# A two-layer diffusion step on one core: weight loads and modulation loads in buffers of their own, and where the dot products stand

## The chip, the core and the metric

The kernel runs on one core of one Trainium2 chip. Five engines matter here: TensorE (PE in the rows; PEld is its weight load), VectorE (DVE), ScalarE (ACT), GpSimd (POOL) and SyncE (SP), whose only work is to issue loads. Each engine takes its instructions in program order and waits on semaphores. The metric is the device time of one execution, in microseconds (us), the median of several runs. GB in rates are 10^9 bytes; a MiB is 1,048,576 bytes.

## The reference

One step of a backbone with two layers, on 128 context tokens and 128 latent tokens, all in float32. D_MODEL is 2048 and D_FF 5632. What each layer computes:

```
m = silu(cond) @ w_mod_l + b_mod_l          # shift1, scale1, gate1, shift2, scale2, gate2
h = rms_norm(x) * (1 + scale1) + shift1
q_r, k_r, v_r, g_r, q_a, k_a, v_a = split(h @ w_in_l)     # 8 retention heads, 8 attention heads on 2 key heads
y = concat(retention_output(...), attention(...))
x = x + gate1 * (y @ w_out_l)
h = rms_norm(x) * (1 + scale2) + shift2
x = x + gate2 * ((silu(gate) * val) @ w_down_l)           # gate, val: depthwise conv of h @ w_up_l
```

The modulation m has six vectors of 2048 for each layer and token kind, so w_mod is 2 x 2048 x 12288 numbers: it is read once, for two columns of cond. After both layers there is one more norm with a gain. Outputs are the tokens and the new key, value and state caches.

## The kernel before

**Pieces.** All 256 tokens stay on chip, transposed. `build_work` (L47) cuts the four weight matrices of each layer into 128x128 tiles and lists them in the order of use, in 768 pieces of eight tiles (`PIECE`). For a piece, `split_upto` (L461) makes hi (ACT, L469) and lo (DVE, L470) from the raw float32 tiles, and `triple` (L635) multiplies each tile three times (L637 to L639), so a piece is 24 matmuls of 256 columns. Splits run `LOOK` = 3 pieces ahead of PE, in four hi and four lo buffers.

**Stages.** In layer 0, pieces 0 to 47 form the wide start (eight head groups by quarters of the contraction), 48 to 87 finish the heads, 88 to 119 are the output projection, 120 to 383 the feed-forward block in thirds (up, down, three times). Layer 1 follows from 384, its output projection is 472 to 503. Beside the heads, attention and retention run as side tasks, a step after each piece (`kv_task`, `q_task`, `ret_task`), with small matmuls into tiles named aux.

**Modulation** is computed in two ways. On PE: `emit_mod` (L394) and `emit_modq` (L377) multiply cond with one unit of w_mod of 1 MiB into a tile md; units come in pairs. `QSTART` are the 32 units at the start, `PESEQ` 32 units in layer 0, `QMID` 16 units, and `QNORM` four units at each of three norms, between the parts of the norm. On DVE: `emit_dot` (L407) multiplies a 1 MiB unit with cond and sums along the row, once for each token kind (k = 0 and 1), so a unit has two dots; it writes its product to the tile hua, by which the rows name it. `DVESEQ` lists the 100 units that go this way.

**What sets the order.** `body` first writes a list of events: each piece, and after it the modulation units that `quota` (L168, from the table `knots`) grants, and the dots that `plan` grants. `plan` spreads the dots evenly up to their due piece over the pieces whose `room` is not zero: all from piece 48 on (`ahead`), without those around a norm. Then the list is emitted in that order on all engines.

**Loads.** `need` (L257) lists all loads, weights and modulation, in the order of first use, and `pump` (L315) issues them on SP in that order, into five buffers (`RAWB`) of 1 MiB: a weight unit is sixteen tiles (`UNIT`), that is two pieces. A buffer comes free in `done` (L339), when its last reader has been emitted, and the load that takes it waits on SP for that reader; loads behind it on SP wait too.

Of the kernel before, what the change touches and what calls it, by code (L numbers as in the profile page):

```python
# [8 lines left out]
F32 = mybir.dt.float32  # L9
# [6 lines left out]
P = 128  # L16
D = 2048
KC = D // P
# [7 lines left out]
UNIT = 16  # L26
LOOK = 3
RAWB = 5
THIRDS = ((0, 16), (16, 16), (32, 12))
# [88 lines left out]

MU = KC * KC // UNIT

# [13 lines left out]
def body(ctx: ExitStack, tc: tile.TileContext, io):  # L134
    nc = tc.nc
# [119 lines left out]
    loads, where = [], {}  # L255

    def need(key):  # L257
        if key not in where:
            where[key] = len(loads)
            loads.append(key)  # L260

    sp = 0
    for ev, arg in events:
        if ev in ("mod", "modq"):
            need((ev, arg))
        elif ev == "dot":
            need(("dot", arg[:3]))
        elif ev in ("presplit", "piece"):
            upto = min(arg[0] + LOOK + 1 if ev == "piece" else arg, len(pieces))
            while sp < upto:  # L270
                need(("main", pieces[sp]["u"]))
                sp += 1
# [3 lines left out]
    wp = ctx.enter_context(tc.tile_pool(name="wp", bufs=RAWB))  # L276
    sp_ = ctx.enter_context(tc.tile_pool(name="split", bufs=LOOK + 1))
# [35 lines left out]
    raw, consumed, nload = {}, [0] * len(loads), [0]  # L313

    def pump():  # L315
        while nload[0] < len(loads):
            i = nload[0]
            if len(raw) >= RAWB:
                return
            key = loads[i]  # L320
            t = wp.tile([P, UNIT * P], F32, tag="raw", name="raw")
            if key[0] == "main":
                u = units[key[1]]
                n = u["n"] * P
                src = io[u["key"]][u["off"] * P * P:(u["off"] + u["n"]) * P * P]
                nc.sync.dma_start(t[:, :n], src.rearrange("(p f) -> p f", p=P))
            else:
                src = io["w_" + key[0]]
                if key[0] == "dot":
                    at = (DVESEQ.index(key[1]),)  # L330
                else:
                    at = ((PESEQ if key[0] == "mod" else QSEQ).index(key[1][:-1]), key[1][-1])
                for i in at:
                    src = src[i]
                nc.sync.dma_start(t, src)
            raw[key] = t
            nload[0] += 1

    def done(key):  # L339
        consumed[where[key]] = 1  # L340
        del raw[key]
        pump()
# [134 lines left out]
    def square(kc):  # L477

        x = xT[:, kc, :]
        if kc == 0:  # L480
            nc.scalar.activation(ssq, x, AF.Square)
        else:
            t = tp.tile([P, 256], F32, tag="t1", name="sq", bufs=4)
# [19 lines left out]
    def norm1():  # L503
        ps = aux()
        for s in range(2):
            for t in (ssq, diag[0]):
                nc.tensor.matmul(ps[:, s:s + 1], t[:, P * s:P * s + P], mean, start=t is ssq, stop=t is not ssq)
        ms = tp.tile([P, 2], F32, tag="ms", name="ms")
        nc.vector.tensor_scalar_add(ms, ps[:, 0:2], EPS)
        rs = tp.tile([P, 2], F32, tag="rs", name="rs")  # L510
        nc.gpsimd.tensor_tensor(rs, ms, mhalf, op=ALU.pow)
        dg = tp.tile([P, 256], F32, tag="t1", name="dg", bufs=4)
# [12 lines left out]
    def emit_hu(l, w, kcs, ahead=True):  # L525

        m = modT[l]
        for kc in kcs:
            if ahead:
                u = hua[:, kc % 4, :]  # L530
            else:
                u = tp.tile([P, 256], F32, tag="t1", name="hu", bufs=4)
# [228 lines left out]
    def layer_tables(l):  # L761
# [7 lines left out]
        for h in range(NH):  # L769
            t = tp.tile([P, 256], F32, tag="t1", name="dtmp", bufs=4)[:, 0:P]  # L770
# [121 lines left out]
    def ret_task(l, h, r):  # L892
# [53 lines left out]
        yf = tp.tile([P, 256], F32, tag="t1", name="ry", bufs=4)  # L946
# [65 lines left out]
def layout(inputs):  # L1012
# [18 lines left out]
    arrays["w_modq"] = np.stack([wm[l, :, :, :, v, b].transpose(0, 2, 1, 3).reshape(MU // 4, P, UNIT * P) for l, v, b in QSEQ])  # L1031
    wm = a["w_mod"].reshape(DEPTH, MU, KC // MU, P, 6, D)
    arrays["w_mod"] = np.stack([wm[l, :, :, :, v].transpose(0, 2, 1, 3).reshape(MU, P, UNIT * P) for l, v in PESEQ])
# [75 lines left out]
```

## Time and profile before

| | |
|---|---|
| median of 3 runs | 2460.34 us (2458.66 to 2462.38) |
| the profiled execution | 2464.25 us, of which its span 2462.4 us |
| PE busy | 2389.6 us (97%), 19730 instructions |
| DVE busy | 1842.0 us (75%) |
| ACT busy | 1201.9 us (49%) |
| moved by DMA | 619.38 MB, mean 252 GB/s |
| mean granted PE clock | 0.99 |
| DMA in the 40 slices, GB/s, first nine | 394 333 314 235 272 261 341 372 292 |

Half of the loads are weights (384 of 1 MiB), a quarter is modulation (192 of 1 MiB). Each slice is 61.6 us. A busy share is a mean over stages with different limits, so the stages are read one by one below. Pieces are counted by the matmuls of one line, eight to a piece.

### The profile page before, as it was taken

Reading aid. Unit: us, or ns where it says so; the run is one execution under the profiler, and the core shown is the slowest. Engines: PE = TensorE matmul, PEld = TensorE weight load, DVE = VectorE, ACT = ScalarE, POOL = GpSimd, SP = SyncE. Lnnn points to the kernel's source line nnn. Section 1 sums busy time; section 2 is a strip of 40 time slices with the busy share of each in tenths; the row PEclk is TensorE's granted clock in tenths of the full one; section 3 lists DMA queues with packets and bytes.
Section 4 is the critical chain, followed back from the end, with each engine's and each line's share of the span. In section 5 each row is a group of like instructions: output and inputs, shape, how many; then the busy total and the mean of one; then the engine's idle time right before and its main releaser. Section 6 shows DMA issues by size and latency. Waiting matters only on the chain.

```text
span 2462.4 us, 46787 instructions
## 1 busy us (share of the span) xinstructions
PE 2389.6 (97%) x19730; PEld 2289.1 (93%) x19730; DVE 1842.0 (75%) x2484; ACT 1201.9 (49%) x1896; POOL 24.7 (1%) x29
## 2 busy tenths in 40 slices
PE   6999989999999999999999999999999999999998
PEld 4888778789999999999989899998999999999997
DVE  4567777669998999889996878796997456655665
ACT  4534433355544555445556544456554454544554
POOL 0000000000000000000000000000000000000000
PEclk9999999999999999999999999999999999999999
DMA  9886778976777777777775687876676555555552
GB/s 394 333 314 235 272 261 341 372 292 239 258 272 261 266 260 258 272 262 264 262 270 208 217 296 289 297 272 227 226 286 217 185 185 187 189 182 187 185 183 86
DMA packets 91266, 619.38 MB, mean 252 GB/s; under 512 B 10160, under 2 KB 16304, under 8 KB 16944
## 3 DMA queue, kind: packets, MB, share of 16 engines
q1 hardware_dynamic: 83520, 605.21, 67.6%
q10 hardware_dynamic: 7536, 11.19, 1.2%
q8 instruction: 154, 2.52, 0.4%
q14 instruction: 56, 0.46, 0.0%
HBM read 611.64 MB, written 4.72 MB: 250 GB/s over the span
## 4 chain that ended last, share of the span: by engine, by line
PE 86%; DVE 6%; DMA 5%; ACT 2%; issue 1%; SPq 0%; POOL 0%; ACTq 0%; DVEq 0%; POOLq 0%
PE acc L637 27%; PE acc L639 27%; PE acc L638 27%; DMA raw<-in_w_modq 2%; DVE lo L470 2%; PE md L387 2%; DMA raw<-in_w_mod 2%; DVE hua L410 2%; ACT hi L469 1%; PE md L401 1%; ACT pr L833 1%; DMA raw<-in_w_in 0%; PE aux L861 0%; DVE st L825 0%; PE aux L442 0%
## 5 line engine op out<-in xcount | busy, mean ns | idle before, releaser
L470 DVE TENSOR_TENSOR lo<-raw,hi 128x1024 fp32r<-128x1024 f32 x768 | 934.6, 1222 | 373.2 <-ACT hi L469 370.3
L637 PE MATMUL acc<-hT,hi 128*128 128x256 f32 x4224 | 1203.0, 285 | 6.5 <-ACT hT L564 6.5
L638 PE MATMUL acc<-hT,hi 128*128 128x256 f32 x4224 | 1183.3, 280 | 0.8 <-DVE hT L569 0.8
L639 PE MATMUL acc<-hT,lo 128*128 128x256 f32 x4224 | 1182.7, 280 | 0.0
L469 ACT CAST hi<-raw 128x1024 fp32r<-128x1024 f32 x768 | 806.0, 1051 | 698.7 <-PE acc L638 585.8
L637 PEld LDWEIGHTS acc<-hT,hi 128*128 128x128 f32 x4224 | 797.8, 189 | 33.8 <-issue 18.3
L638 PEld LDWEIGHTS acc<-hT,hi 128*128 128x128 f32 x4224 | 795.5, 188 | 3.2 <-DVE hT L569 1.2
L639 PEld LDWEIGHTS acc<-hT,lo 128*128 128x128 f32 x4224 | 798.3, 189 | 0.0
L639 PE MATMUL acc<-ypair,lo 128*128 128x256 f32 x1920 | 543.7, 283 | 2.7 <-DVE lo L470 2.7
L637 PE MATMUL acc<-ypair,hi 128*128 128x256 f32 x1920 | 545.8, 284 | 0.0
L638 PE MATMUL acc<-ypair,hi 128*128 128x256 f32 x1920 | 543.3, 283 | 0.1
L410 DVE SCALAR_TENSOR_TENSOR hua<-raw,cbc 128x2048 bf16<-128x2048 f32 x200 | 456.7, 2284 | 6.6 <-DMA raw<-in_w_dot 6.6
L637 PEld LDWEIGHTS acc<-ypair,hi 128*128 128x128 f32 x1920 | 368.4, 192 | 8.6 <-issue 6.7
L639 PEld LDWEIGHTS acc<-ypair,lo 128*128 128x128 f32 x1920 | 368.3, 192 | 3.4 <-DVE lo L470 3.3
L638 PEld LDWEIGHTS acc<-ypair,hi 128*128 128x128 f32 x1920 | 368.4, 192 | 0.4 <-DVE ypair L758 0.3
L717 ACT ACTIVATE gx<-acc,modT 128x128 f32<-128x128 f32 x240 | 68.6, 369 | 94.8 <-PE acc L639 94.8
L719 DVE TENSOR_TENSOR xT<-gx,xT 128x512 f32<-128x512 f32 x60 | 41.4, 691 | 72.4 <-ACT gx L717 72.4
L387 PE MATMUL md<-raw,sc 128*32 128x512 f32 x480 | 65.8, 654 | 24.5 <-DMA raw<-in_w_modq 14.5
L746 DVE SCALAR_TENSOR_TENSOR cv<-acc,cst,cv 128x254 f32<-128x254 f32 x176 | 84.8, 482 | 6.2
L737 ACT ACTIVATE cv<-acc,cst 128x256 f32<-128x256 f32 x176 | 89.4, 558 | 0.0
L744 DVE SCALAR_TENSOR_TENSOR cv<-acc,cst,cv 128x254 f32<-128x254 f32 x176 | 83.4, 474 | 0.0
L387 PEld LDWEIGHTS md<-raw,sc 128*32 128x32 f32 x480 | 11.9, 113 | 53.1 <-DMA raw<-in_w_modq 28.4
(130 smaller groups left out, 922.7 us busy)
## 6 DMA issues: line engine op xcount, KB each, us to landing
raw<-in_w_up SPq DMA_DIRECT2D x176, 1024.0 KB, 4.9
raw<-in_w_dot SPq DMA_DIRECT2D x100, 1024.0 KB, 6.3
raw<-in_w_in SPq DMA_DIRECT2D x88, 1024.0 KB, 6.8
raw<-in_w_down SPq DMA_DIRECT2D x88, 1024.0 KB, 4.9
raw<-in_w_modq SPq DMA_DIRECT2D x60, 1024.0 KB, 7.0
raw<-in_w_mod SPq DMA_DIRECT2D x32, 1024.0 KB, 8.7
raw<-in_w_out SPq DMA_DIRECT2D x32, 1024.0 KB, 5.8
xT<-in_xT ACTq DMA_DIRECT2D x2, 1024.0 KB, 10.2
```

The lines of the kernel that those rows point to most:

```text
L387: nc.tensor.matmul(md[0][32 * j:32 * j + 32, :], sc[:, 2 * kc:2 * kc + 32], t[:, 512 * i:512 * i + 512], start=kc < 4, stop=kc >= 12)
L410: nc.vector.scalar_tensor_tensor(hua.rearrange("p c t -> p (c t)").bitcast(BF16), raw[key], 1.0, acc[:, k, :], op0=ALU.mult, op1=ALU.mult, ...
L469: nc.scalar.copy(hi, r)
L470: nc.vector.tensor_tensor(lo, r, hi.bitcast(F32), op=ALU.subtract)
L637: nc.tensor.matmul(out, hi, src[:, 0:256], start=first, stop=False, skip_group_check=True)
L638: nc.tensor.matmul(out, hi, src[:, 256:512], start=False, stop=False, skip_group_check=True)
L639: nc.tensor.matmul(out, lo, src[:, 0:256], start=False, stop=last, skip_group_check=True)
L717: nc.scalar.activation(tv[:, i, P * s:P * s + P], pv[:, i, P * s:P * s + P], AF.Copy, scale=modT[l][:, v, nt + i, s:s + 1])
L719: nc.vector.tensor_tensor(xT[:, nt:nt + 2, :], tv, xT[:, nt:nt + 2, :], op=ALU.add)
L737: nc.scalar.activation(t, src, AF.Identity, bias=C("convb", l * 2 * FC + f, 1), scale=w)
L744: nc.vector.scalar_tensor_tensor(t[:, :, 1:P], src[:, :, 0:P - 1], w[0], t[:, :, 1:P], op0=ALU.mult, op1=ALU.add)
L746: nc.vector.scalar_tensor_tensor(t[:, :, 0:P - 1], src[:, :, 1:P], w[2], t[:, :, 0:P - 1], op0=ALU.mult, op1=ALU.add)
```

## The change

Weight units shrink from sixteen tiles to eight (0.5 MiB, one piece) and keep their five buffers in the pool `wp`. Modulation units keep 1 MiB and get a pool of their own, `vp`, with three buffers (`MODB`), in tiles named vec. `pump` keeps two lists and fills the modulation buffers first; no weights are loaded before eight modulation units have been issued. To make room, the small temporaries of tag t1 go from four buffers to three (seven places, not shown again below). Dots start only at the output projection of layer 0 (`gstart["out", 0]`, piece 88). Four of their units (quarter 1 of layer 0's scale2, eight dots) go to PE: one more entry of `QMID`, four units, and the table `knots` grants them.

```diff
-UNIT = 16
+UNIT = 8
+MUNIT = 16
 LOOK = 3
 RAWB = 5
+MODB = 3
...
-QMID = [(0, 4, 0), (1, 2, 1), (1, 2, 2), (1, 2, 3)]
+QMID = [(0, 4, 0), (0, 4, 1), (1, 2, 1), (1, 2, 2), (1, 2, 3)]
...
-DVESEQ = [(l, v, u) for l, v, n in ((0, 4, 4), (0, 5, 4), (1, 1, 0), (1, 0, 0), (1, 4, 0), (1, 3, 0), (1, 5, 4))
+DVESEQ = [(l, v, u) for l, v, n in ((0, 4, 8), (0, 5, 4), (1, 1, 0), (1, 0, 0), (1, 4, 0), (1, 3, 0), (1, 5, 4))
...
-    knots = [(ahead, 0), (gstart["out", 0] - 2, MU), (gstart["up", 0] - 4, 9 * MU // 4), (gstart["kv", 1] + 16, 9 * MU // 4),
-             (gstart["out", 1] - 2, 3 * MU)]
+    knots = [(ahead, 0), (gstart["out", 0] - 2, MU), (gstart["up", 0] - 4, 5 * MU // 2), (gstart["kv", 1] + 16, 5 * MU // 2),
+             (gstart["out", 1] - 2, 13 * MU // 4)]
...
-        if j >= ahead and not ends:
+        if j >= gstart["out", 0] and not ends:
             room[j] = DSHARE[g["kind"]]
...
-    loads, where = [], {}
+    loads = {"main": [("main", i) for i in range(len(units))], "mod": []}
...
+    vp = ctx.enter_context(tc.tile_pool(name="vp", bufs=MODB))
...
-    raw, consumed, nload = {}, [0] * len(loads), [0]
+    raw, nload, held = {}, {"main": 0, "mod": 0}, {"main": 0, "mod": 0}
 
     def pump():
-        while nload[0] < len(loads):
-            i = nload[0]
-            if len(raw) >= RAWB:
-                return
...
+        while nload["mod"] < len(loads["mod"]) and held["mod"] < MODB:
+            key = loads["mod"][nload["mod"]]
+            t = vp.tile([P, MUNIT * P], F32, tag="vec", name="vec")
...
+        while nload["main"] < len(units) and held["main"] < RAWB and nload["mod"] >= MU // 2:
+            i = nload["main"]
+            u = units[i]
+            n = u["n"] * P
             t = wp.tile([P, UNIT * P], F32, tag="raw", name="raw")
...
     def done(key):
-        consumed[where[key]] = 1
+        held["main" if key[0] == "main" else "mod"] -= 1
         del raw[key]
         pump()
```

How loads stand on SP in the middle of layer 0's output projection, before (in_w_mod and in_w_modq are units for PE, in_w_dot units for DVE, in_w_out weights):

```order
L335 DMA raw<-in_w_mod 128x2048 x2
L326 DMA raw<-in_w_out 128x2048
L335 DMA raw<-in_w_dot 128x2048
L326 DMA raw<-in_w_out 128x2048
L335 DMA raw<-in_w_mod 128x2048 x2
L326 DMA raw<-in_w_out 128x2048
L335 DMA raw<-in_w_mod 128x2048 x2
```

The same place now:

```order
L323 DMA vec<-in_w_dot 128x2048
L323 DMA vec<-in_w_mod 128x2048 x2
L333 DMA raw<-in_w_out 128x1024 x3
L323 DMA vec<-in_w_mod 128x2048 x2
L323 DMA vec<-in_w_dot 128x2048
L333 DMA raw<-in_w_out 128x1024 x2
L323 DMA vec<-in_w_mod 128x2048 x2
```

Between two pairs for PE there stood one or two MiB of weights and at times a dot unit; now there stand two or three pieces of half a MiB, and a dot unit more often.

SP at the end of layer 1's output projection, where the norm takes four units (in_w_modq x4), before:

```order
L326 DMA raw<-in_w_out 128x2048 x3
L335 DMA raw<-in_w_dot 128x2048
L326 DMA raw<-in_w_up 128x2048 x2
L335 DMA raw<-in_w_modq 128x2048 x4
L326 DMA raw<-in_w_up 128x2048 x8
```

and now:

```order
L323 DMA vec<-in_w_modq 128x2048
L333 DMA raw<-in_w_out 128x1024 x3
L333 DMA raw<-in_w_up 128x1024 x2
L323 DMA vec<-in_w_modq 128x2048
L333 DMA raw<-in_w_up 128x1024 x6
L323 DMA vec<-in_w_modq 128x2048 x2
L323 DMA vec<-in_w_dot 128x2048 x2
```

The first two of the four units now stand ahead of weights of the next stage, the last two behind eight pieces of them.

DVE in a retention head of layer 0 (L936 sends a variance to POOL, L940 uses what comes back), before:

```order
L923 SCALAR_TENSOR_TENSOR ro<-aux,dec,ro 128x128 x2
L933 BN_STATS bs<-ro 128x6 x2
L935 BN_AGGR ag<-bs 128x2 x2
L936 TENSOR_SCALAR grs<-ag 128x2
L410 SCALAR_TENSOR_TENSOR hua,modT<-raw,cbc 128x2048
L470 TENSOR_TENSOR lo<-raw,hi 128x1024
L940 TENSOR_SCALAR ro<-ro,ag,grs 128x128 x2
```

and now:

```order
L922 SCALAR_TENSOR_TENSOR ro<-aux,dec,ro 128x128 x2
L932 BN_STATS bs<-ro 128x6 x2
L934 BN_AGGR ag<-bs 128x2 x2
L935 TENSOR_SCALAR grs<-ag 128x2
L469 TENSOR_TENSOR lo<-raw,hi 128x1024
L939 TENSOR_SCALAR ro<-ro,ag,grs 128x128 x2
```

The dot between the two is gone, and with it all 17 dots of pieces 48 to 87. After pieces 88 to 115 there are now 17 dots where there were 13, and 22 units for PE where there were 18; in the first up stage (pieces 136 to 183) there are 23 dots where there were 20. All later stages keep their numbers within one.

## Rows read from the trace of the kernel before

**Rows 1.** Stages: start:end, length; busy PE, PEld, DVE, ACT, POOL; clock, DMA share, GB/s.

```profile
33.20:204.20 171.00, 168.00 (x1368) 147.16 (x1369) 106.21 (x183) 78.97 (x110) 0.00 (x0) 0.97 0.88 334
204.20:386.90 182.70, 167.70 (x1298) 146.62 (x1296) 136.65 (x242) 74.03 (x144) 6.75 (x7) 0.98 0.68 251
386.90:497.70 110.80, 103.51 (x843) 87.37 (x840) 73.32 (x90) 41.24 (x72) 0.69 (x1) 1.00 0.96 374
571.70:707.40 135.70, 135.70 (x1155) 135.70 (x1154) 131.96 (x175) 71.22 (x101) 0.00 (x0) 1.00 0.74 264
```

**Rows 2.** The same view for line L639 alone: eight matmuls are one piece.

```profile
386.90:497.70 110.80, 63.14 (x224) 42.86 (x224) 1.00 0.96 374
799.50:980.50 181.00, 142.94 (x513) 96.25 (x512) 1.00 0.72 261
```

**Rows 3.** DVE in the dots (L410) alone, by stage; each dot has two records.

```profile
204.20:386.90 182.70, 36.66 (x32) 0.98 0.68 251
```

**Rows 4.** Timeline of the start: start, length, engine, line, operation, [idle before <- releaser].

```profile
29.08 1.07 PE L387 MATMUL md<-raw,sc 128*32 128x512 f32 x8 [1.42 <-DMA raw<-in_w_modq]
31.55 1.04 ACT L469 CAST hi<-raw 128x1024 fp32r<-128x1024 f32 x1 [0.75 <-DMA raw<-in_w_in]
31.77 0.17 DVE L371 TENSOR_TENSOR modT<-modT,cst 128x8 f32<-128x8 f32 x1
33.24 0.38 PE L637 MATMUL acc<-hT,hi 128*128 128x256 f32 x1 [1.73 <-ACT hT L564]
```

**Rows 5.** Timeline of the wide start around 65 us: loads issued, and PE's units.

```profile
54.92 0.80 SPq L335 DMA_DIRECT2D raw<-in_w_modq  x2
55.73 0.35 ACTq L425 DMA_DIRECT2D cbc<-in_cb  x1
64.89 1.06 PE L387 MATMUL md<-raw,sc 128*32 128x512 f32 x8
67.83 1.94 PE L387 MATMUL md<-raw,sc 128*32 128x512 f32 x8 [1.88 <-DMA raw<-in_w_modq]
```

**Rows 6.** Waits of PE in 204.2 to 386.9: who waited for whom, sum, times, longest.

```profile
PE aux L945 <- DVE ro L940: 5.8, 5, 2.2
PE aux L861 <- ACT pt L850: 2.7, 3, 1.8
PE aux L848 <- DVE pr L841: 2.6, 1, 2.6
```

**Rows 7.** Timeline of one retention head in that stretch.

```profile
336.30 2.28 DVE L410 SCALAR_TENSOR_TENSOR hua<-raw,cbc 128x2048 bf16<-128x2048 f32 x1
339.65 0.60 DVE L940 TENSOR_SCALAR ro<-ro,ag,grs 128x128 f32<-128x128 f32 x2
340.13 0.49 PE L945 MATMUL aux<-cst,ro 128*128 128x128 f32 x2 [2.15 <-DVE ro L940]
340.55 3.35 PE L401 MATMUL md<-raw,sc 128*32 128x512 f32 x16
```

**Rows 8.** Layer 0's output projection: PE's wait; bytes moved in 386.9 to 497.7.

```profile
PE md L401 <- DMA raw<-in_w_mod: 7.0, 6, 1.6
DMA packets 6114, 41.47 MB, mean 374 GB/s; under 512 B 684, under 2 KB 1113, under 8 KB 1113
```

**Rows 9.** Busy time by stage, 5 to 50 us, when loads queue without a gap.

```profile
5.00:50.00 45.00, 30.21 (x190) 17.23 (x191) 21.64 (x59) 19.52 (x40) 0.69 (x1) 0.92 1.01 421
```

**Rows 10.** Chain of waits: a load issued with nothing queued ahead, issue to landing.

```profile
1280.92 4.82 DMA raw<-in_w_modq
```

**Rows 11.** Timeline of the norms before layer 1 and before its feed-forward block.

```profile
1281.13 1.92 PE L387 MATMUL md<-raw,sc 128*32 128x512 f32 x16
1285.79 1.06 PE L387 MATMUL md<-raw,sc 128*32 128x512 f32 x8 [0.29 <-DMA raw<-in_w_modq]
1684.00 1.92 PE L387 MATMUL md<-raw,sc 128*32 128x512 f32 x16
1690.74 1.94 PE L387 MATMUL md<-raw,sc 128*32 128x512 f32 x8 [2.84 <-DMA raw<-in_w_modq]
```

More of the change, by code (lines that the diff above doesn't have):

```diff
@@ L252, in body @@
     events.append(("norm2", None))
-    loads, where = [], {}
+    loads = {"main": [("main", i) for i in range(len(units))], "mod": []}
     def need(key):
[L258 to L262, printed above, removed]
+        if key not in loads["mod"]:
+            loads["mod"].append(key)
     for ev, arg in events:
@@ L267, in body @@
             need(("dot", arg[:3]))
[L268 to L272, printed above, removed]
     one = ctx.enter_context(tc.tile_pool(name="one", bufs=1))
     wp = ctx.enter_context(tc.tile_pool(name="wp", bufs=RAWB))
+    vp = ctx.enter_context(tc.tile_pool(name="vp", bufs=MODB))
     sp_ = ctx.enter_context(tc.tile_pool(name="split", bufs=LOOK + 1))
@@ L310, in body @@
     modT = {}
-    raw, consumed, nload = {}, [0] * len(loads), [0]
+    raw, nload, held = {}, {"main": 0, "mod": 0}, {"main": 0, "mod": 0}
     def pump():
-        while nload[0] < len(loads):
-            i = nload[0]
-            if len(raw) >= RAWB:
-                return
-            key = loads[i]
-            t = wp.tile([P, UNIT * P], F32, tag="raw", name="raw")
[L322 to L337, printed above, removed]
+        while nload["mod"] < len(loads["mod"]) and held["mod"] < MODB:
+            key = loads["mod"][nload["mod"]]
+            t = vp.tile([P, MUNIT * P], F32, tag="vec", name="vec")
+            src = io["w_" + key[0]]
+            if key[0] == "dot":
+                at = (DVESEQ.index(key[1]),)
+            else:
+                at = ((PESEQ if key[0] == "mod" else QSEQ).index(key[1][:-1]), key[1][-1])
+            for i in at:
+                src = src[i]
+            nc.sync.dma_start(t, src)
+            raw[key] = t
+            nload["mod"] += 1
+            held["mod"] += 1
+        while nload["main"] < len(units) and held["main"] < RAWB and nload["mod"] >= MU // 2:
+            i = nload["main"]
+            u = units[i]
+            n = u["n"] * P
+            t = wp.tile([P, UNIT * P], F32, tag="raw", name="raw")
+            src = io[u["key"]][u["off"] * P * P:(u["off"] + u["n"]) * P * P]
+            nc.sync.dma_start(t[:, :n], src.rearrange("(p f) -> p f", p=P))
+            raw["main", i] = t
+            nload["main"] += 1
+            held["main"] += 1
     def done(key):
-        consumed[where[key]] = 1
+        held["main" if key[0] == "main" else "mod"] -= 1
         del raw[key]
@@ L482, in square @@
         else:
-            t = tp.tile([P, 256], F32, tag="t1", name="sq", bufs=4)
+            t = tp.tile([P, 256], F32, tag="t1", name="sq", bufs=3)
             nc.scalar.activation(t, x, AF.Square)
@@ L511, in norm1 @@
         nc.gpsimd.tensor_tensor(rs, ms, mhalf, op=ALU.pow)
-        dg = tp.tile([P, 256], F32, tag="t1", name="dg", bufs=4)
+        dg = tp.tile([P, 256], F32, tag="t1", name="dg", bufs=3)
         nc.vector.tensor_scalar_mul(dg[:, 0:P], ident, rs[:, 0:1])
@@ L531, in emit_hu @@
             else:
-                u = tp.tile([P, 256], F32, tag="t1", name="hu", bufs=4)
+                u = tp.tile([P, 256], F32, tag="t1", name="hu", bufs=3)
             hu[kc] = u
@@ L769, in layer_tables @@
         for h in range(NH):
-            t = tp.tile([P, 256], F32, tag="t1", name="dtmp", bufs=4)[:, 0:P]
+            t = tp.tile([P, 256], F32, tag="t1", name="dtmp", bufs=3)[:, 0:P]
             nc.vector.tensor_scalar(Dt[:, h, :], C("diff"), 0.0, C("lgd", 2 * l * NH + h, 1), op0=ALU.max,
@@ L945, in ret_task @@
             nc.tensor.transpose(ps[:, P * s:P * s + P], o[:, s, :], ident)
-        yf = tp.tile([P, 256], F32, tag="t1", name="ry", bufs=4)
+        yf = tp.tile([P, 256], F32, tag="t1", name="ry", bufs=3)
         nc.vector.scalar_tensor_tensor(yf, ps[:, 0:256], C("gn", l * NH + h, 1), r[:, 3, :], op0=ALU.mult,
@@ L1030, in layout @@
     wm = a["w_mod"].reshape(DEPTH, MU // 4, 4 * KC // MU, P, 6, 4, 512)
-    arrays["w_modq"] = np.stack([wm[l, :, :, :, v, b].transpose(0, 2, 1, 3).reshape(MU // 4, P, UNIT * P) for l, v, b in QSEQ])
+    arrays["w_modq"] = np.stack([wm[l, :, :, :, v, b].transpose(0, 2, 1, 3).reshape(MU // 4, P, MUNIT * P) for l, v, b in QSEQ])
     wm = a["w_mod"].reshape(DEPTH, MU, KC // MU, P, 6, D)
-    arrays["w_mod"] = np.stack([wm[l, :, :, :, v].transpose(0, 2, 1, 3).reshape(MU, P, UNIT * P) for l, v in PESEQ])
+    arrays["w_mod"] = np.stack([wm[l, :, :, :, v].transpose(0, 2, 1, 3).reshape(MU, P, MUNIT * P) for l, v in PESEQ])
     wm = a["w_mod"].reshape(DEPTH, D, 6, KC, P)
```

2 lines of the change are left out of this document (1 added, 1 removed).

## The prediction

> **What bounds the kernel now.** I read the stages first. In an up stage PE is busy all the time: 64 pieces in 181.0 us [rows 2], 2.83 us a piece, and no load is waited for. All up and down stages look like this, so a faster load or a lighter DVE buys nothing there. PE loses time in three places. In the wide start (33.2 to 204.2) it idles 171.0 - 168.0 = 3.0 us at a mean granted clock of 0.97; in the heads of layer 0 (204.2 to 386.9) 182.7 - 167.7 = 15.0 us at 0.98; in layer 0's output projection (386.9 to 497.7) 110.8 - 103.5 = 7.3 us [rows 1]. The waits say on whom. In the heads it is DVE and ACT, the engines beside PE [rows 6]. In the output projection 7.0 us are waits of a unit for its load [rows 8]; that stretch moves 374 GB/s with its DMA engines 0.96 busy [rows 1], and when loads queue without a gap they move 421 [rows 9]. So there two limits lie close together: PE's work of 103.5 us, and 41.47 MB, which at 421 GB/s take 98.5 us. The change takes work from the heads' DVE and puts bytes into this projection. That is the exchange to be weighed.
>
> **Start and wide start.** The first half-unit of weights is on chip half a MiB sooner: at 421 GB/s a MiB takes 2.49 us, so 1.24 us before the 31.55 of the first cast. The first matmul also waits for the shift that DVE finishes at 31.94 [rows 4], so of 1.24 I count 0.5 us gained. Then five pieces (2.5 MiB) stand ahead of the ninth unit, where 2 MiB stood: 1.24 us later, of which I take 1.0 as lost, between 0 and 1.2. At 64.89 a pair of units runs, and its second half starts at 67.83 after a wait of 1.88 us; it also runs at half speed, 1.94 us for 1.06 [rows 5], and the next eight or so matmuls cost 0.21 us instead of 0.12. Together about 1.9 + 0.9 + 0.9 = 3.7 us. Both units of that pair were issued at 54.92, at the same time as the 2 MiB tile cbc on ACT's queue. With three buffers of its own, the first of the pair is issued a pair earlier, and only the second at about 55, where the first lies now and lands in time. Gain 3.7, bounds 0 and 5. Sum here: -0.5 + 1.0 - 3.7 = -3.2.
>
> **Heads of layer 0 without dots.** The 17 dots there are 36.66 us [rows 3] of DVE's 136.65 [rows 1]. DVE isn't full (75%), so the gain isn't 36.66. What counts is a dot that stands between a result and PE's wait for it: at 336.30 a dot of 2.28 us stands ahead of L940, PE waits 2.15 us, and the pair of units after it takes 3.35 us instead of 1.92, because the clock had fallen [rows 7, 11]. Of PE's waits in this stretch DVE ends 5.8 + 2.6 = 8.4 us [rows 6]. The clock of 0.98 means twice 2% of 182.7 us at the lower of its two levels, 1.2 GHz, a loss of 3.65 us; half of it goes with the waits. 8.4 + 1.8 = 10.2, and I take 10. Bounds: 4, if only the two heads gain where a dot stands right ahead of L940, and 15.0 + 3.65 = 18.6, if PE never waits.
>
> **Layer 0's output projection.** The stretch is 28 pieces [rows 2]. It gets four more units and four more dots, which are two units: 6 MiB, 6.29 MB. PE's part is four units of 0.96 us (1.92 a pair [rows 11]): 103.5 + 3.9 = 107.4 us. The loads are 41.47 + 6.29 = 47.76 MB, less half a MiB more that the larger buffers hold at the start: 47.2 MB. At 374 GB/s, the rate of this stretch, that is 126.3 us; at 394, the mean of the page's first slice, 119.9; at 421, 112.2. So the loads become the bound. I take 394: the buffers will be empty more often than before, which keeps the loads queued, but each pair is issued only when a buffer falls free, which leaves gaps. 119.9 - 110.8 = +9, bounds +1.4 and +15.5. DVE's nine more microseconds there lie beside this (73.3 of 110.8 busy), as do the four transposes that close one more group of units.
>
> **The norms.** Each takes two units, does a part of the norm, and takes two more. At the second norm of layer 1 a dot unit is half used and holds the third buffer, so the third unit is issued when the first is used up, at 1684.96, and lands 4.82 us later with nothing ahead of it [rows 10], at 1689.8; the fourth 2.49 later, at 1692.3. Before, it started at 1690.74 [rows 11]. Loss 1.5 us. At the norm before layer 1 the third buffer is free; the fourth unit is issued at 1282.1 and lands at 1286.9, with a piece of weights ahead at 1288.1, against 1285.79: 1.5. In layer 0's second norm the same reckoning gives 5.8 us from first to fourth, and 0.5 lost. Sum +3.5, bounds 1 and 6.
>
> **Edits that cost nothing.** In the first up stage DVE is 131.96 of 135.70 us busy [rows 1]; three more dots make 138.8, which is 3.1 too many. Splits run three pieces, 8.5 us, ahead of PE, so the debt is covered until the down stage: 0.5, bounds 0 and 3.1. Twice as many weight loads keep SP busy for 768 issues instead of 384, and it does little else. Three t1 buffers instead of four delay at most the eight heads' last step; I count 0, bound 3.
>
> **The sum.** -3.2 - 10 + 9 + 3.5 + 0.5 = -0.2 us on the profiled 2464.25. That execution lies 3.9 us above the median of the runs, so the forecast for the median is 2460.34 - 0.2 = 2460.1, call it 2460.
>
> **Rivals.** *Loads keep their queue full.* If the two rings keep DMA at 421 GB/s, the projection loses 1.4 instead of 9, and the heads, with DVE at 100 of 182 us, may give 12: -0.5 - 3.7 - 12 + 1.4 + 3.5 = -11.3, 2449 us. For it: 45 us at 421 at the start [rows 9], and separate rings can't block each other's turn. Against: there five 1 MiB loads were always waiting.
> *Three buffers are too few.* A pair of units is issued when the pair before is used up, and needs 4.82 + 2.49 = 7.3 us; pairs come every two or three pieces, 5.7 or 8.5 us. If that leaves DMA gaps as now, at 374 GB/s, the projection loses 15.5, and the heads give 6 only: -0.5 + 1.0 - 3.7 - 6 + 15.5 + 3.5 + 3.1 = +12.9, 2473 us, slower. It decides once the projection moves less than about 385 GB/s.
> *Dots were not what held the heads.* Attention's chain goes through ACT, and the fourteen other dots stand where nobody waits. Then the 10 becomes 2, and the time is 2468.
> *Half-sized loads pay twice.* A lone MiB takes 4.82 us, 2.33 more than its 2.49 in a queue. If each load paid that, the projection's 14 MiB of weights would cost 14 more such parts: +32.6, 2493 us. Against it: the queue of rows 9 hides this part already. The Trainium skill, "DMA: Bandwidth & Descriptors", section "Bandwidth", says to batch transfers to 1 MiB or more for 75% of the peak, which speaks against half-MiB weights. By that rule this rival would hold; its figure is for single transfers, and the trace's 421 GB/s with queued ones shows the rule doesn't bind while several are in flight.
>
> **How the numbers follow.** Forecast 0.36; full queue 0.34; three too few 0.18; dots not the cause 0.08; half-sized loads 0.04. A measurement of this kernel tells 0.2% (4.9 us) from no change. Faster is the second case and an edge of the first, 0.36; the same 0.34; slower 0.30. The range goes from 2447, just beyond the full queue, to 2474, just beyond the three buffers, and leaves out the last case and the ends of the bounds. Within 0.2%, the forecast's own range is 2455 to 2465.
>
> **What would show it.** The wide start: no wait for a unit near 65 us. The heads: PE's waits for L940's successor gone, the stretch from the first head to the first piece of the projection 10 us shorter. The projection: its 28 pieces at 120 us, with waits for vec loads ahead of units and a rate near 394 GB/s. The norms: the fourth unit's wait longer by 1 to 2 us. The up stages: still 2.83 us a piece. I am wrong if the projection isn't held by loads, if PE's waits in the heads stay, or if an up stage slows down.

## The result: slower, and the profile after

The changed kernel takes 2491.73 us (median of 4 runs, 2489.31 to 2495.11), the kernel before in the same session 2459.5 (4 runs): ratio 1.0135, 95% interval 1.0112 to 1.0159, some 33 us slower. The forecast was no change, with 2474 as the upper end. The profiled executions (2489.31 after, 2464.25 before) differ by 25.1 us; it is these that the stages below divide.

Piece starts are read from the matmuls of the trace. Only stages that moved by 0.5 us or more are listed.

| stage | before, us | after, us | difference | forecast |
|---|---|---|---|---|
| heads of layer 0 (pieces 48 to 87) | 182.7 | 173.9 | -8.8 | -10 |
| output projection of layer 0, 28 pieces | 110.8 | 127.2 | +16.4 | +9 |
| pieces 116 to 119, with the norm | 25.9 | 34.0 | +8.1 | +0.5 |
| first up stage | 135.7 | 138.2 | +2.5 | +0.5 |
| last down part, with the norm before layer 1 | 80.8 | 87.4 | +6.7 | +1.5 |
| heads of layer 1 | 251.9 | 249.8 | -2.1 | 0 |
| output projection of layer 1, with its norm | 106.0 | 110.1 | +4.1 | +1.5 |
| 16 pieces after each of two norms | 95.8 | 93.6 | -2.2 | 0 |

Start and wide start came out even (+0.4 and -0.4), where -3.2 was forecast. All other up and down stages are unchanged at 2.83 us a piece.

Busy time by stage after; columns as in [rows 1]. The stages are the wide start, the heads, the 28 pieces, pieces 116 to 119, and the first up stage:

```profile
33.70:204.30 170.60, 166.61 (x1369) 147.21 (x1370) 106.29 (x183) 79.09 (x110) 0.00 (x0) 0.98 0.91 342
204.30:378.20 173.90, 164.55 (x1298) 144.81 (x1296) 103.41 (x210) 74.07 (x144) 4.83 (x7) 1.00 0.66 224
378.20:505.30 127.10, 113.43 (x877) 91.51 (x876) 82.67 (x102) 42.80 (x74) 2.60 (x1) 0.95 0.94 358
505.30:539.30 34.00, 23.94 (x160) 15.96 (x158) 14.02 (x24) 9.11 (x18) 0.69 (x1) 0.81 0.90 346
586.90:725.10 138.20, 137.68 (x1155) 136.41 (x1154) 137.18 (x179) 67.78 (x100) 0.00 (x0) 1.00 0.75 260
```

Against [rows 1], in the heads DVE has 33 us less to do, PE idles 9.35 us for 15.0, and its clock is full. In the 28 pieces PE idles 13.7 us for 7.3, the clock falls to 0.95, and the rate falls from 374 to 358 GB/s although more has to be moved: the DMA engines aren't busier than before, they are a little less busy. In the first up stage DVE is now busy for all but 1 us of 138.2.

The waits of PE in the heads, then those of DVE and PE in the whole output projection (sum, times, longest):

```profile
PE aux L944 <- DVE ro L939: 3.9, 5, 0.9
...
DVE hua L409 <- DMA vec<-in_w_dot: 24.4, 7, 5.4
PE md L386 <- DMA vec<-in_w_modq: 12.7, 5, 4.0
```

The first line answers to [rows 6] (5.8 us). The second is new in size: DVE waits 24.4 us there for dot units that haven't landed; over the whole page the same line has 27.1. Before, the same stretch had

```profile
DVE hua L410 <- DMA raw<-in_w_dot: 5.5, 2, 4.3
```

What a late dot does. The chain of waits (start, us, what), then the timeline of DVE, PE and SP, a little after 395:

```profile
394.25 1.04 PE md L400 x8
...
395.31 7.71 DMA vec<-in_w_dot
...
403.12 0.12 DVE hua L409
```

```profile
403.12 2.29 DVE L409 SCALAR_TENSOR_TENSOR hua<-vec,cbc 128x2048 bf16<-128x2048 f32 x1 [4.24 <-DMA vec<-in_w_dot]
405.34 1.22 DVE L469 TENSOR_TENSOR lo<-raw,hi 128x1024 fp32r<-128x1024 f32 x1
...
407.45 0.58 PE L636 MATMUL acc<-ypair,hi 128*128 128x256 f32 x1 [4.10 <-ACT ypair L756]
...
398.39 8.52 SPq L333 DMA_DIRECT2D raw<-in_w_out  x2
```

The dot's unit is issued only when PE has used up a unit and given back its buffer (394.25 + 1.04), and takes 7.71 us to land. DVE stands still for 4.24 us, with the next lo and the retention head's ry queued behind the dot; PE runs dry for 4.10 us and then starts slower (0.58 us for this matmul, 0.28 for those ahead of the wait). SP, meanwhile, issues two loads in 8.52 us: the second waits for a buffer that DVE's lo is to free, and whatever stands behind it on SP waits too. One late dot thus delays DVE, PE and the next loads.

What happens at a norm, here the one before layer 1 (timeline of PE and SP, then the chain; compare [rows 11]):

```profile
1295.38 0.33 SPq L323 DMA_DIRECT2D vec<-in_w_modq  x1
1296.52 3.98 SPq L333 DMA_DIRECT2D raw<-in_w_in  x3
1297.38 1.92 PE L386 MATMUL md<-vec,sc 128*32 128x512 f32 x16
1300.55 0.43 SPq L323 DMA_DIRECT2D vec<-in_w_modq  x1
1308.74 1.94 PE L386 MATMUL md<-vec,sc 128*32 128x512 f32 x8 [5.44 <-DMA vec<-in_w_modq]
```

```profile
1293.15 2.21 DVE hua L409 x2
...
1300.55 8.15 DMA vec<-in_w_modq
```

The third unit is issued at 1295.38, when DVE has finished the dot that held the third buffer (1293.15 + 2.21). The first unit is used up about 1298.4; the fourth could be issued then, but SP is inside three weight loads that wait for their own buffers, and gets to it at 1300.55. With those half-MiB loads ahead of it the unit lands 8.15 us later, not 4.82 as the lone one of [rows 10]. Piece 383, which holds this norm, takes 19.0 us for 10.9; pieces 119 and 503 take 15.6 for 13.3 and 18.4 for 14.4.

### The profile page after: what moved, and what is told of

It reads as the page before. It is cut to its first block, busy times and chain, and to the rows that moved or that the text cites. A ratio compares the mean times of both kernels' runs of the same rounds, so it can differ in the third digit from the quotient of the medians.

```text
span 2487.5 us, 47728 instructions
## 1 busy us (share of the span) xinstructions
PE 2399.8 (96%) x19766; PEld 2292.3 (92%) x19766; DVE 1826.2 (73%) x2471; ACT 1199.1 (48%) x1897; POOL 22.7 (1%) x29
## 4 chain that ended last, share of the span: by engine, by line
PE 82%; DVE 7%; DMA 5%; issue 3%; ACT 2%; SPq 0%; POOL 0%; DVEq 0%; POOLq 0%; ACTq 0%
PE acc L636 26%; PE acc L638 25%; PE acc L637 25%; DVE lo L469 3%; DMA vec<-in_w_modq 3%; PE md L386 2%; DVE hua L409 1%; PE md L400 1%; DMA vec<-in_w_mod 1%; ACT hi L468 1%; DMA raw<-in_w_in 1%; DMA vec<-in_w_dot 1%; PE aux L860 0%; DVE cv L743 0%; ACT pr L832 0%
## 5 line engine op out<-in xcount | busy, mean ns | idle before, releaser
L409 DVE SCALAR_TENSOR_TENSOR hua<-vec,cbc 128x2048 bf16<-128x2048 f32 x192 | 438.7, 2285 | 27.1 <-DMA vec<-in_w_dot 27.1
L386 PE MATMUL md<-vec,sc 128*32 128x512 f32 x512 | 72.4, 672 | 44.5 <-DMA vec<-in_w_modq 44.4
L386 PEld LDWEIGHTS md<-vec,sc 128*32 128x32 f32 x512 | 12.9, 114 | 75.5 <-DMA vec<-in_w_modq 48.3
```

Source lines behind the costliest of these rows:

```text
L386: nc.tensor.matmul(md[0][32 * j:32 * j + 32, :], sc[:, 2 * kc:2 * kc + 32], t[:, 512 * i:512 * i + 512], start=kc < 4, stop=kc >= 12)
L409: nc.vector.scalar_tensor_tensor(hua.rearrange("p c t -> p (c t)").bitcast(BF16), raw[key], 1.0, acc[:, k, :], op0=ALU.mult, op1=ALU.mult, ...
```

## Experiments

Each ratio is against the kernel before in the same session; its medians lie between 2459.5 and 2462.95 us. The changed kernel was run in the first session only, so a difference of two medians against it can be off by some 3 us.

**The two halves alone.** The first kernel has the change's two rings with the schedule of before; the second has one ring of five 1 MiB buffers with the change's schedule.

```diff
 # rings_only, against the changed kernel
-QMID = [(0, 4, 0), (0, 4, 1), (1, 2, 1), (1, 2, 2), (1, 2, 3)]
+QMID = [(0, 4, 0), (1, 2, 1), (1, 2, 2), (1, 2, 3)]
...
-        if j >= gstart["out", 0] and not ends:
+        if j >= ahead and not ends:
```

> The rings of the change (five half-MiB weight buffers, three modulation buffers), but the schedule of before: dots in layer 0's heads, 20 units for PE before the norm. Theory S (the loss comes from the schedule, 6 MiB more in layer 0's output projection): the 28 pieces of that stretch stay near 111 us, the heads near 183; only the norms lose, so about 2470 us. Theory R (three modulation buffers are too few, whatever the schedule): the stretch takes 120 us or more and the norms lose too, about 2485 us.

```diff
 # sched_only, against the kernel before
-QMID = [(0, 4, 0), (1, 2, 1), (1, 2, 2), (1, 2, 3)]
+QMID = [(0, 4, 0), (0, 4, 1), (1, 2, 1), (1, 2, 2), (1, 2, 3)]
...
-        if j >= ahead and not ends:
+        if j >= gstart["out", 0] and not ends:
```

> The one ring of five 1 MiB buffers of before, with the schedule of the change (no dots in layer 0's heads, one more QMID entry, its table). Theory S: heads 9 us shorter, the stretch of 28 pieces 125 us or more, norms as before: about 2468 us. Theory R: heads 9 us shorter, the stretch about 115 us, norms as before: about 2455 us.

Rings alone: 2478.1 us, ratio 1.0062 (1.0047 to 1.0078), about 15 us slower. Its heads (182.9) and its 28 pieces (110.4) are as before; pieces 119, 383 and 503 take 17.2, 17.8 and 19.1 us, 15.5 more than before: the rings lose at the norms. Schedule alone: 2465.34, ratio 1.0012 (1.0000 to 1.0024), about 3 us slower. Its heads gain 8.3 us and its 28 pieces lose 12.9; the exchange that the prediction weighed comes out a little negative, without any rings. Both parts lose, and together they lose some 14 us more than the sum of the two by the medians, 9.6 in the profiled executions. There 8.5 of it lies in layer 0's output projection: its 28 pieces lose 16.4 us with both and 12.4 as a sum, pieces 116 to 119 lose 8.1 and 3.6. DVE's waits for dot units there are 5.5 us before, 11.1 with the rings alone, 15.9 with the schedule alone, 24.4 with both.

**The late dots.** The changed kernel, where layer 0's scale2 dots read a tile that is on chip, while their units are loaded and given back by GpSimd (that part of the modulation is not computed); then the same without loading those eight units.

```diff
+    junk = one.tile([P, 2], F32, name="junk")
...
+        own = (l, v) != (0, 4)
-        nc.vector.scalar_tensor_tensor(hua.rearrange("p c t -> p (c t)").bitcast(BF16), raw[key], 1.0, acc[:, k, :],
+        nc.vector.scalar_tensor_tensor(hua.rearrange("p c t -> p (c t)").bitcast(BF16), raw[key] if own else acc[:, 0, :],
+                                       1.0, acc[:, k, :],
...
+            if not own:
+                nc.gpsimd.tensor_tensor(junk, raw[key][:, 0:2], mhalf, op=ALU.mult)
```

> The changed kernel, but the dots of layer 0's scale2 read a resident tile instead of their loaded unit (so that part of the modulation isn't computed); the units are still loaded, and GpSimd reads two columns to release them. Bytes, order and DVE's work are the same; DVE alone no longer waits for these loads. If DVE waiting for a late dot unit (24 us there), with splits behind it, is what stretches the projection, the 28 pieces fall from 127 to about 115 us and the total to about 2480. If bytes or PE's own units are what is late, nothing changes: 2488 to 2492.

```diff
 # dots_unloaded: besides own and the read of the resident tile above
-        elif ev == "dot":
+        elif ev == "dot" and arg[:2] != (0, 4):
...
-        if k == 1:
+        if k == 1 and own:
```

> The changed kernel; layer 0's scale2 dots read a resident tile and their eight units are not loaded at all (that part of the modulation is not computed). Against the run where these dots don't wait but are loaded (2481.7 us, 28 pieces of the projection in 120.0 us, 45.35 MB): the projection carries some 8 MB less. Theory A, bytes bound the stretch once the dots' waits are gone: 120.0 falls to PE's work, about 109 to 111 us, and the whole to about 2471 us. Theory B, the PE units' own latency with three buffers in pairs bounds it: 118 to 120 us stay, 2479 to 2482 us. The units also get the buffers that the dots held, so a fall below 115 us speaks for bytes or buffers together, no fall against both.

Without the wait: 2481.68 us, ratio 1.0076 (1.0061 to 1.0091); the 28 pieces take 120.0 us at 378 GB/s, 7 less, with the same loads. So late dots cost PE time, here about a third of what DVE waits for them. The norms stay as they are (15.9, 19.0, 18.4). Without the loads: 2468.9, ratio 1.0029 (1.0017 to 1.0041), theory A. The window of the 28 pieces there:

```profile
380.30:487.40 107.10, 107.02 (x877) 88.74 (x876) 82.53 (x102) 42.72 (x74) 2.60 (x1) 1.00 0.94 356
```

PE is busy for all of it, at the full clock. So PE's own work is 107.0 us (forecast 107.4), and what stood above it was loads: bytes, or buffers that dots held.

**A fourth buffer.** To tell bytes from buffers, the modulation gets four buffers and the weights three, in the same space.

```diff
-RAWB = 5
-MODB = 3
+RAWB = 3
+MODB = 4
```

> The changed kernel with four buffers for units and dots instead of three, and three half-MiB buffers for weights instead of five (the same 5.5 MiB). Theory A, the ring of three is what costs: a norm's four units are then in flight at once, so pieces 119, 383 and 503 come back from 15.5, 19.0 and 18.4 us to within 2 us of the 13.4, 10.9 and 14.4 of the kernel before, 10 to 14 us in all; and DVE's waits for late dots in the output projection fall from 24.4 us to less than half, which returns about the 7 us of its 28 pieces that the run without late dots returned: 2471 to 2475 us. Theory B, the units come late because they are queued behind weight loads on the one issuing engine, however many buffers there are: the waits stay or move to the weights, 2488 to 2495 us. In either, up and down stages at 2.83 us a piece would show that three half-MiB weight buffers are enough.

2514.47 us, ratio 1.021 (1.0195 to 1.0226): neither theory's time, since three half-MiB weight buffers are too few elsewhere. The first up stage takes 154.8 us, the wide start ends at 211.4. But in the projection it answers; the window of its 28 pieces, then DVE's wait for dot units and, from the first up stage, ACT's for weights:

```profile
385.60:500.10 114.50, 110.25 (x878) 90.71 (x877) 82.35 (x102) 42.96 (x74) 2.60 (x1) 0.97 0.98 394
```

```profile
DVE hua L409 <- DMA vec<-in_w_dot: 5.2, 4, 2.5
...
ACT hi L468 <- DMA raw<-in_w_up: 31.0, 21, 3.6
```

With the same loads, half-MiB weights among them, the stretch now moves 394 GB/s and takes 114.5 us for 127.2; pieces 116 to 119 take 23.4 for 34.0, and piece 119 takes 9.9. The same 5.5 MiB can be under way in both, so it was neither that space nor half-MiB weights as such, but the division into buffers that held the rate at 358. The run changes both numbers at once; DVE's wait for dots, 5.2 us for 24.4, speaks for the fourth modulation buffer, but a run with that change alone is missing. Pieces 383 and 503 stay at 17.7 and 18.4 us, which theory A didn't expect. There the units are landed now, and another wait has come in (timeline of piece 383; L487 is the sum of squares for the norm):

```profile
1318.72 2.29 DVE L409 SCALAR_TENSOR_TENSOR hua<-vec,cbc 128x2048 bf16<-128x2048 f32 x1
1326.71 0.51 PE L506 MATMUL aux<-mean,ssq 128*128 128x1 f32 x2 [3.71 <-DVE ssq L487]
1328.43 3.64 PE L386 MATMUL md<-vec,sc 128*32 128x512 f32 x16
```

A dot, and splits of weights that come late, stand on DVE ahead of the sums, which is read from this timeline and not tested; PE waits 3.71 us and runs the two last units in 3.64 us where 1.92 is full speed.

**Fewer units in the projection.** Eight of its PE units go to the heads, with the change's rings, and with one ring (there also four).

```diff
-    knots = [(ahead, 0), (gstart["out", 0] - 2, MU), ...
+    knots = [(ahead, 0), (gstart["out", 0] - 2, 3 * MU // 2), ...
```

> The changed kernel with eight PE units moved from layer 0's output projection into its heads, by one number of the table (24 instead of 16 units granted by the end of the heads). No byte is added or removed. Theory S: the stretch of 28 pieces falls from 127 us by about 8 MiB at 2.5 to 2.9 us, to 105 to 110, the heads grow by PE's 8 us: net 10 to 14 us faster than the changed kernel, about 2480. Theory R: the pairs and dots still wait for their buffers; the stretch falls only by PE's 8 us, the total stays near 2491.

> One ring of five 1 MiB buffers as before, the schedule of the change (no dots in layer 0's heads), and eight of TensorE's units moved from the output projection to the heads. Theory A, the heads have room for units but the projection has none for bytes, whatever the rings: the heads go from 174.4 to about 182 us as they did with the change's rings, the 28 pieces from 123.7 to about 107 (PE 101 busy): 2465.3 + 8 - 17 = 2456 us, ratio about 0.997. Theory B, the shift paid only because it relieved the ring of three: the projection gives back about 8, what the heads take: 2464 to 2467 us.

> As the run with eight units moved, with four moved. Theory A (bytes of the projection): half of the gain, 2460 us, if the projection is held by loads to the end; if it becomes PE-bound already after four units, as much as with eight or more, 2455 us, since the heads take only 4 us. Theory B (relief of the ring of three only): 2464 to 2466 us.

On the rings 2478.1 us, ratio 1.006 (1.0043 to 1.0077), 13.6 us less than the change: the heads go back to 182.2 us, the 28 pieces to 109.3. On one ring with eight 2456.91, ratio 0.9986 (0.9974 to 0.9998), heads 182.4, 28 pieces 106.2; with four 2459.91, 0.9994 (0.9984 to 1.0004), 178.0 and 114.6. Theory A holds: eight units cost the heads 8 us and give back 17 to 18 in the 28 pieces, rings or not. The heads have room in DMA (251 GB/s in [rows 1], 224 after); the projection hasn't. The units don't fill PE's idle time in the heads: that is 9.35 us in the change and 9.35 with eight units more.

**The norms.** First, weights that would have come after a norm's units in the one list are held back on their ring until the units are issued; second, the planner's window without dots begins 12 instead of 4 pieces ahead of a norm.

```diff
 # gate: gate[i] counts the modulation loads up to the last norm unit ahead of weight unit i in the order of before
-        while nload["main"] < len(units) and held["main"] < RAWB and nload["mod"] >= MU // 2:
+        while nload["main"] < len(units) and held["main"] < RAWB and nload["mod"] >= max(MU // 2, gate[nload["main"]]):
```

> The changed kernel, with the weights' ring held back at the three norms: a piece of weights that the kernel before would have issued after a norm's four units waits until all four are issued. Theory A, the rings let weights overtake the units: the norm's fourth unit, now 8 to 8.8 us from issue to landing with up to three half-MiB weight loads ahead, lands after about 5 us; PE's wait of 5.4 us at piece 383 falls to about 2, and pieces 119, 383 and 503 (15.6, 19.0, 18.4 us) lose 2 to 4 us each: 2480 to 2486 us. Theory B, the fourth unit is late because its buffer comes free only when the first unit is used: it is issued no earlier, and what it lands earlier the first pieces after the norm wait for their weights: no change, 2489 to 2493 us.

```diff
 # early
-        ends = any(gstart[k] - 4 < j <= gstart[k] + 12 for k in QNORM)
+        ends = any(gstart[k] - 12 < j <= gstart[k] + 12 for k in QNORM)
```

> The changed kernel, with the planner's window without dots begun 12 instead of 4 pieces ahead of a norm (two dots fewer in layer 0's output projection, two more in the first up stage). Theory A, a dot that holds the third buffer until 1 to 3 us before the norm makes the third unit late, and its 2.29 us on DVE stands ahead of the norm's sums of squares: the third unit is issued some 10 us earlier, the wait for the sums (1.7 us at piece 383) goes, the fourth unit still waits for the first one's buffer: pieces 383 and 503 lose 2 to 5 us each, piece 119 about 1, and the projection's 28 pieces about 3 for 1 MiB less: 2480 to 2486 us. Theory B, only the number of buffers counts: the fourth unit sets the end, piece 383 loses at most the 1.7 us, and the whole is 2486 to 2491 us.

Held back: 2480.82 us, ratio 1.0078 (1.0064 to 1.0091), theory A. Pieces 119, 383 and 503 fall to 13.5, 13.4 and 16.2. At piece 383 (timeline of SP and PE; lines are 9 further down in this kernel):

```profile
1293.25 3.46 SPq L332 DMA_DIRECT2D vec<-in_w_modq  x2
1296.80 2.53 SPq L342 DMA_DIRECT2D raw<-in_w_in  x5
...
1300.02 3.43 PE L395 MATMUL md<-vec,sc 128*32 128x512 f32 x16
```

The third and fourth unit are issued one behind the other within 3.46 us, the weights after them, and the last two units run without a wait for the fourth. So the same three buffers lose 5.6 us less at this norm when weights don't overtake the units. The 28 pieces lose 1.8 us by it (129.0).

A wider window: 2488.4 us, ratio 1.0105 (1.0091 to 1.0119), a time of theory B. Pieces 383 and 503 fall to 14.5 and 14.3 us, as theory A has it, but piece 119 takes 16.2 for 15.6, and the total hardly falls, since the projection's dots now stand earlier: its 28 pieces take 135.2 us at 345 GB/s, 8 more, where 3 less were expected. Sixteen dots now stand in 20 pieces, where 18 stood in 28; that their closer spacing meets the ring of three again is the likely reason, and only argued.

**All together on the rings**, first with both changes at the norms and eight units moved, then without the wider window:

> The changed kernel with all three repairs: eight PE units moved to the heads, dots kept 12 pieces ahead of a norm, weights held back at the norms. If the three add up (13.6 for the units by the run with them alone, 6 to 10 for each of the others by theory A of their runs): 2456 to 2466 us, and what is left above the kernel before is the fourth unit of three norms. If the norms' loss is that of the three buffers alone: 2474 to 2478 us, as with the eight units alone.

> The changed kernel, eight PE units moved to the heads and weights held back at the norms, with the planner's window as in the change. If the two repairs add up (13.6 and 10.9 us by their own runs): 2467 us, and pieces 119, 383 and 503 at 13.4 to 16.2 us as with the weights held back alone, the 28 pieces at 109 us. What is left above the kernel before, 4 to 5 us, would then be the start on separate buffers (2 to 3 us later) and DVE's full first up stage (2.5). If the weights held back cost the projection its rate once it has fewer units: 2472 to 2476 us.

2475.03 us, ratio 1.0056 (1.004 to 1.0071), near the second reading, but for another reason: its norms are short (13.4, 13.5, 13.5), its 28 pieces take 116.5 us instead of 109.3. Without the wider window 2468.19, ratio 1.0034 (1.0021 to 1.0047): the two repairs do add up, and 8 us above the kernel before are left. Of these the first up stage has 2.4 (138.1 us). Another part is the start: the wide start ends between 204.3 and 208.4 us in the nine profiles with rings of five and three, at 206.2 in the mean, and between 201.4 and 204.2, at 202.6, in the six with one ring.

**What the one ring gives.** The wider window on the one ring, with the change's schedule and eight units moved; and alone on the kernel before.

> One ring of five 1 MiB buffers, the schedule of the change, eight PE units moved to the heads (2456.9 us), and the dots kept 12 pieces ahead of a norm. With five buffers a parked dot leaves four for a norm's units, so the buffer theory expects nothing at the norms from it, only the 1 MiB less in layer 0's output projection (0 to 2 us, as its 28 pieces are near PE's own work) against two more dots in a first up stage that DVE already fills (2 us lost): 2455 to 2459 us. If a dot ahead of the norm's sums costs by DVE's time, pieces 383 and 503 fall by 1 to 2 us each, from 12.5 and 14.7: 2452 to 2455 us.

> The kernel before, with only the planner's window without dots begun 12 instead of 4 pieces ahead of a norm. Theory A, the norms' last microseconds hang on dots that hold a buffer and stand on DVE just ahead of a norm: pieces 119, 383 and 503 (13.3, 10.9, 14.4 us) fall to 9.9 each as in the fastest kernel, 8.8 us in all, and layer 0's output projection gets 3 dots fewer, 1 to 3 us: 2451 to 2453 us. Theory B, the norms were short there only because the change's schedule had also moved units and dots: no change at piece 119 and at most 3 us at the others: 2458 to 2462 us.

2449.26 us, ratio 0.9947 (0.9935 to 0.996), the fastest kernel of this study; alone 2454.43, ratio 0.9977 (0.9966 to 0.9987). In the first, pieces 119, 383 and 503 take 9.9 us each, for 13.3, 10.9 and 14.4 before; in the second 9.9, 9.9 and 13.5. Piece 383 of the fastest kernel (timeline of SP and PE):

```profile
1269.04 0.33 SPq L335 DMA_DIRECT2D raw<-in_w_modq  x1
1271.85 1.93 PE L387 MATMUL md<-raw,sc 128*32 128x512 f32 x16
1274.69 1.92 PE L387 MATMUL md<-raw,sc 128*32 128x512 f32 x16
```

The last unit is issued before the first is used, both pairs run whole, and PE waits for no load. The reading I had written down for five buffers, that a parked dot leaves enough of them and the norms gain nothing, is wrong, and the other one, 1 to 2 us at two norms, was too small: 2449.26 lies below both. The window alone takes 5.2 us off the three pieces of the kernel before, so dots in the last pieces ahead of a norm did cost there. It is less than the 8.8 of its theory A, as piece 503 stays at 13.5, and the 1 to 3 us that layer 0's output projection was to gain did not come (111.7). Some 6 us of the fastest kernel's nearly 14 come from the window alone, the rest from the schedule of the change with the projection relieved.

## Why the prediction was wrong

*Start and wide start, -3.2.* Wrong by sign over all profiles. The stall at 65 us went as forecast. But the first piece begins 0.4 us later, not 0.5 sooner: the eight units at the start now pass through three buffers too, which the forecast left out, and the last of them runs at 30.04 instead of 29.08 [rows 4]. And PE's second unit after the first piece comes late (timeline of PE after, then before):

```profile
27.57 1.10 PE L386 MATMUL md<-vec,sc 128*32 128x512 f32 x8
30.04 1.06 PE L386 MATMUL md<-vec,sc 128*32 128x512 f32 x8 [1.37 <-DMA vec<-in_w_modq]
...
39.59 1.07 PE L386 MATMUL md<-vec,sc 128*32 128x512 f32 x8 [0.52 <-DMA vec<-in_w_modq]
43.58 1.07 PE L386 MATMUL md<-vec,sc 128*32 128x512 f32 x8 [2.92 <-DMA vec<-in_w_modq]
```

```profile
39.63 2.35 PE L387 MATMUL md<-raw,sc 128*32 128x512 f32 x16
```

I had taken the later ninth unit at 1.0 us of queue time; behind it the tenth is later still. The chain of waits after shows how:

```profile
23.48 7.79 DMA raw<-in_w_in
...
31.29 0.03 SPq L323
...
31.34 12.19 DMA vec<-in_w_modq
```

The buffer of the tenth unit comes free at 28.67 (27.57 + 1.10), but SP issues it at 31.34, when the first load of weights has landed (23.48 + 7.79). In the traces each load reports on one of eight semaphores, taken in turn, and SP waits for the load that had it before. In the nine profiles with rings of five and three, six to eight issues of the first 78 us start within 0.1 us of such a landing; with one ring none does. With four modulation buffers and three for weights the last start unit runs at 29.46, the first piece begins at 33.1, and the pair is whole again, at 39.24. In the changed kernel's own profile all this just eats the gain at 65 us; over all profiles the wide start ends 3.6 us later on the rings.

*Heads, -10.* Right in the sum, -8.8, and in part by luck. DVE's 33 us were mostly hidden, as forecast. But PE's idle time fell by 5.7 us where 8.4 were put down, and its wait for `ro` is not gone, 3.9 us for 5.8; the clock, back at full, took 3.2 us off PE's busy time (167.70 to 164.55, the same matmuls) where 1.8 were put down.

*Projection, +9, bounds 1.4 to 15.5.* This step failed, at +16.4, beyond its upper bound, and pieces 116 to 118, for which nothing was forecast, lost another 5.9. PE's work was right (107.0 against 107.4), and the bytes were a little too many (45.55 MB measured for 47.2). What failed is the rate, "the buffers will be empty more often than before, which keeps the loads queued". A free buffer is worth nothing if the load that is to fill it stands behind another that waits on SP, or if the buffer is held by a dot that DVE can't start. At 394 GB/s, the rate I took, 45.55 MB are 115.6 us; the kernel with four buffers did 114.5 at 394. With three it was 358. And "DVE's nine more microseconds there lie beside this" counted busy time only: a dot that waits 4.24 us for its unit blocks DVE, which works in order, and with it the splits. Taking these waits away gave back 7 us.

*Norms, +3.5, bounds 1 to 6.* Failed by the most: the three pieces took 14.4 us more. The step was the time from issue to landing, 4.82 us from [rows 10] with at most one piece of weights ahead, and, before layer 1, a third buffer that was taken to be free. At piece 383 a dot held that buffer until the norm, SP was inside weight loads when the buffer of the first unit fell free, and the fourth unit then took 8.15 us with those loads ahead. At piece 503 the buffers went as forecast: the third and fourth unit were issued when the first two were used. But they took 7.2 and 8.79 us to land, behind weight loads that SP had issued just before (timeline of SP and PE, then the chain):

```profile
1692.40 14.03 SPq L333 DMA_DIRECT2D raw<-in_w_up  x6
1707.74 1.19 SPq L323 DMA_DIRECT2D vec<-in_w_modq  x2
1714.99 1.94 PE L386 MATMUL md<-vec,sc 128*32 128x512 f32 x8 [5.47 <-DMA vec<-in_w_modq]
```

```profile
1708.60 8.79 DMA vec<-in_w_modq
```

On one list weights behind a norm's units stayed behind them; two rings on one issuing engine gave this order up, and the listing of SP for this norm, ahead of the prediction, shows it: its last two units stand behind eight pieces of weights (and already its second behind two). Holding the weights back returned 10.9 us on the whole, 9.9 of it by the three pieces.

*First up stage, +0.5, bounds 0 to 3.1.* +2.5, inside the bounds: DVE had 137.18 us of work, and the debt did not stay covered.

*Rivals.* "Three buffers are too few" named the mechanism of the projection, and its rate (374) was still too high; its 2473 us lacked the norms. With the norms as measured, 10.9 us more, it would have said 2484. "Half-sized loads pay twice" came nearest in time (2493) and is not the cause: up stages keep 2.83 us a piece on half-MiB weights, and with a fourth buffer the projection moves 394 GB/s with them. The 421 GB/s that the prediction set against it were moved by 1 MiB loads and say nothing on half ones. The Trainium skill, "DMA: Bandwidth & Descriptors", section "Bandwidth", asks for batches of 1 MiB or more; these runs show no loss of rate from half of that while several loads are in flight, 394 GB/s with half-MiB weights for 374 before.

*What stays open.* The 28 pieces of the change fall to 107.2 us without the dots' loads and to 114.5 with a fourth buffer; how much of the 7.3 us between is bytes alone wasn't separated. Of the 8 us left with both repairs, 2.4 are the first up stage and about 3.6 the start; the rest, some 2 us, is near what a comparison can tell. Four modulation buffers beside five for the weights weren't tried.

## What to carry to other kernels

Two rings on one in-order issuing engine are not independent: whichever load waits for its buffer holds up the other ring, and the order of first use, which a single list keeps, is lost just where several units are needed at once. Count a load's time from the moment its buffer falls free, with what stands ahead of it on the issuing engine and in the queue, and count for an in-order engine not only the busy time of moved work but its waits for data, with all that stands behind. Before giving a burst of loads its own buffers, keep other users out of them ahead of the burst: on the kernel before, that alone gave 0.2%, and together with the relieved schedule 0.5%.

## What the runs showed of the hardware

A load of half the size is not twice as quick. The table of DMA issues of the changed kernel (a MiB load halved to 512 KB; the last column is the median time from issue to landing, in us) has

```profile
raw<-in_w_up SPq DMA_DIRECT2D x352, 512.0 KB, 4.3
raw<-in_w_down SPq DMA_DIRECT2D x176, 512.0 KB, 4.3
```

and that of the kernel before has

```profile
raw<-in_w_up SPq DMA_DIRECT2D x176, 1024.0 KB, 4.9
raw<-in_w_down SPq DMA_DIRECT2D x88, 1024.0 KB, 4.9
```

Half the bytes took 0.6 us off the wait, so five half-MiB buffers hold half the bytes for nearly the same wait; with three of them the first up stage lost 19 us. The other surprise is the spread of the start on two rings: the first piece began between 33.1 and 38.9 us in ten profiles, between 33.0 and 33.7 in six with one ring. It goes with the last of the eight start units, which PE runs at 29.5 to 33.9 us on two rings and at 28.7 to 29.4 on one; why it spreads so on two stays open.
